# An attention kernel: fewer self-waits on ScalarE, a cheaper exp in the planner's table, one DMA transpose a head, first K and Q pieces in PSUM banks of their own

The kernel runs on one core of one Trainium2 chip. The metric is device time in microseconds, lower is better.

## The reference

Grouped-query attention: 8 batches, 8 query heads on 2 key/value heads, 1024 positions, head dimension 64, fp32 in and out.

```python
scores = scale * np.matmul(q_group, k_group.transpose(0, 1, 3, 2))
attn = np.exp(scores - scores.max(axis=-1, keepdims=True))
attn = attn / (np.sum(attn, axis=-1, keepdims=True) + 1e-08)
output[:, q_start:q_end] = np.matmul(attn, v_group)
```

## The kernel before

The work is cut into 128 jobs (batch, head, half of the queries) of 8 cells each; a cell is a 128x512 block of transposed scores, so there are 1024. The exponential of a cell is made on one of two engines. On ScalarE ("A" cells) it is the engine's own exponential, two cells a tile (128x1024). On VectorE ("D" cells) it is a bit trick with a quadratic correction, in groups of 8 cells. The maximum is not subtracted; a column of ones in V gives the row sums.

A planner at build time divides the cells and fixes the order of every engine's instructions, with a table of costs. The order is then static.

```python
QK, PV, P1, NORM = 0.216, 0.1225, 0.603, 0.555
EXP = (0.065, 0.4265)               # fixed part, and for each cell of the tile
... PER_JOB, LEAD, RAMP, AHEAD, FIRST_PV = ... 3, 6, 6, 0.08, 2.0
...
def exps(n, cells):                 # one A tile
    pt = pa_pool.tile([128, 2, QBS], BF16, name="pa")     # 28 buffers
    nc.scalar.activation(out=pt[:, 0:m], in_=psum.pop(("A", n))[:, 0:m],
                         func=AF.Exp, scale=scale)
...
def transpose(key, dst, n):         # PIECE = 256: two a head
    rows = slice(n * PIECE, (n + 1) * PIECE)
    nc.sync.dma_start_transpose(out=dst[:, rows], in_=src[rows, :])
...
# first loads: head 0 is turned on TensorE; both halves of K in one PSUM bank
tk = dbanks[0].tile([128, 2, HALF], BF16, name="dps0")
for n, half in enumerate(halves):
    ...                             # casts, transposes
for copy, half in zip((nc.scalar.copy, nc.vector.tensor_copy), halves):
    put_k(0, 0, half)
    copy(out=qT[(0, 0)][:, cols], in_=tq[:, cols])
turn_k(1, slice(0, NHC))
put_k(0, 1, slice(0, NHC))
nc.gpsimd.dma_start(out=ksets[0][hi, 0, 1, :], in_=ksets[0][lo, 0, 0, :])
```

A tile that is written into a used buffer waits for its readers (PE) and for its earlier writer, which is ScalarE itself. With both waits the build puts a separate wait instruction ahead of the exp.

Of the kernel before, what the change touches and what calls it, by code (L numbers as in the profile page):

```python
# [14 lines left out]
GROUP = 8  # L15
POOL_STEPS = ()


def make_plan(nj, nkc):
# [8 lines left out]
    EXP = (0.065, 0.4265)  # L28
    CHAIN = ((0.20, 0.133), (0.20, 0.133), (0.16, 0.27), (0.16, 0.27))
    FROM_PE, FROM_ACT, FROM_DVE, FROM_POOL = 0.26, 0.17, 0.10, 0.15  # L30
    LIVE_A, LIVE_D, PENDING, PER_JOB, LEAD, RAMP, AHEAD, FIRST_PV = 28, 5, 16, 3, 6, 6, 0.08, 2.0
    INF = 1e9
    FIRST_LOAD, EACH_LOAD = 4.5, 4.2
    ops = []
    pe = act = dve = 0.0
    a_free, bank, obank_free = [0.0, 0.0], [0.0, 0.0], [0.0, 0.0]
    todo = [list(range(nkc)) for _ in range(nj)]
    taken = [0] * nj
    job_a = job_d = 0
# [8 lines left out]
    def loaded(j):  # L48
        h = j // 2
        return FIRST_LOAD + EACH_LOAD * (h - 1 if h < 4 else h) if h else 0.0  # L50

    def first_free(slots):
        return min(range(len(slots)), key=lambda s: slots[s])

    while normed < nj:
# [27 lines left out]
        if len(open_jobs) < 2 and next_job < nj:  # L83
            at = min(ready.get(next_job * nkc + c, INF) for c in range(nkc))
            at = max(pe, FIRST_PV, min(obank_free), at)
            if at < INF:
                best = min(best or (INF,), (at, 3 + len(open_jobs), "open", next_job))
        for q, p, kind in ((normq, 0, "norm"), (p1q, 1, "p1"), (chainq, 2, "chain")):
            if q:
                at = q[0][0]  # L90
                if kind != "chain" or q[0][3] not in POOL_STEPS:
                    at = max(dve, at)
                best = min(best or (INF,), (at, p, kind, 0))
# [3 lines left out]
        if kind == "qk":  # L97
# [4 lines left out]
            if not arg:  # L102
                if open_a is None:
                    slot = first_free(a_free)
                    a_id += 1
                    live["A"] += 1
                    open_a = {"slot": slot, "t": a_free[slot], "cells": []}
                    a_free[slot] = INF
                o = open_a
                ops.append((t, "qk", cell, "A", a_id, o["slot"], len(o["cells"])))  # L110
                o["cells"].append(cell)
                home[cell] = ("A", a_id)
                if len(o["cells"]) == 2 or not any(todo[job_a:]):
                    act = max(act, pe + FROM_PE)
                    ops.append((act, "exp", a_id, tuple(o["cells"])))
                    act += EXP[0] + EXP[1] * len(o["cells"])
                    a_free[o["slot"]] = act + FROM_ACT
                    uses[("A", a_id)] = len(o["cells"])
                    for x in o["cells"]:
                        ready[x] = act + FROM_ACT  # L120
                    open_a = None
            else:
                taken[j] += 1
                k = first_free(bank)
                bank[k] = INF
                pending += 1
                ops.append((t, "qk", cell, "D", k, 0, 0))
                p1q.append((pe + FROM_PE, cell, k))
# [7 lines left out]
        elif kind == "pv":  # L136
# [11 lines left out]
            if done:  # L148
                open_jobs.remove(s)
                normq.append((pe + FROM_PE, s))  # L150
# [6 lines left out]
        elif kind == "p1":  # L157
            _, cell, k = p1q.pop(0)
            if not cur:
                d_id += 1  # L160
                live["D"] += 1
            ops.append((t, "p1", cell, k, d_id, len(cur)))
            dve = t + P1
            bank[k] = dve + FROM_DVE
            cur.append(cell)
            home[cell] = ("D", d_id)
            if len(cur) == GROUP:
                chainq.append((dve + FROM_DVE * (0 in POOL_STEPS), d_id, cur, 0))
                cur = []
        elif kind == "flush":  # L170
            chainq.append((dve + FROM_DVE * (0 in POOL_STEPS), d_id, cur, 0))
            cur = []
        else:
            _, g, cells, step = chainq.pop(0)
            ops.append((t, "chain", g, len(cells), step))
            end = t + CHAIN[step][0] + CHAIN[step][1] * len(cells)
            dve = end if step not in POOL_STEPS else dve
            if step + 1 < len(CHAIN):
                at = end
                if (step in POOL_STEPS) != (step + 1 in POOL_STEPS):  # L180
                    at += FROM_POOL if step in POOL_STEPS else FROM_DVE
                chainq.insert(0, (at, g, cells, step + 1))
            else:
                pending -= len(cells)
                uses[("D", g)] = len(cells)
                for x in cells:
                    ready[x] = dve + FROM_DVE
# [4 lines left out]
def kernel(  # L192
# [27 lines left out]
    PIECE = 256  # L220
    WARM = 30
    CAST_GAP = 3.0
    POOL_DMA = 1.0
    scale = 1.0 / math.sqrt(D)
# [10 lines left out]
    for op in plan:  # L235
        if op[1] == "chain" and op[4] in POOL_STEPS:
            starts.setdefault(op[2], []).append(op[0])
# [9 lines left out]
    pa_pool = ctx.enter_context(tc.tile_pool(name="papool", bufs=28))  # L247
# [14 lines left out]

    blank = const_pool.tile([128, 128], BF16)
# [77 lines left out]
    def first_loads():  # L341
# [7 lines left out]
        tk = dbanks[0].tile([128, 2, HALF], BF16, name="dps0")  # L349
        lo, hi = slice(0, D), slice(D, 2 * D)  # L350

        def turn_k(w, half):
            for c in range(NHC)[half]:
                nc.tensor.transpose(  # L354
                    tk[:, w, c * 128 : (c + 1) * 128],
# [4 lines left out]
        def put_k(side, parity, half):  # L360
# [4 lines left out]
                in_=tk[part, side ^ parity, cols],  # L365
# [19 lines left out]
        tq = dbanks[1].tile([128, HALF], BF16, name="dps1")  # L385
        qT[(0, 0)] = qT_pool.tile([128, HALF], BF16, name="qT")
        last_score[0] = keep_warm(WARM)
        for n, half in enumerate(halves):
# [5 lines left out]
            turn_k(0, half)  # L394
            keep_warm(2)
            for c in range(NHC)[half]:
                nc.tensor.transpose(tq[:, c * 128 : (c + 1) * 128], hq[:, c, :], ident)  # L397
# [3 lines left out]
        for copy, half in zip((nc.scalar.copy, nc.vector.tensor_copy), halves):  # L401
            cols = slice(half.start * 128, half.stop * 128)
            put_k(0, 0, half)
            copy(out=qT[(0, 0)][:, cols], in_=tq[:, cols])
        turn_k(1, slice(0, NHC))
        last_score[0] = keep_warm(4)
        put_k(0, 1, slice(0, NHC))
# [5 lines left out]
    temps = {}  # L413
    stage = {}
# [19 lines left out]
    def exps(n, cells):  # L434
        pt = pa_pool.tile([128, 2, QBS], BF16, name="pa")
        m = len(cells)
        nc.scalar.activation(  # L437
            out=pt[:, 0:m], in_=psum.pop(("A", n))[:, 0:m], func=AF.Exp, scale=scale
        )
        for col, cell in enumerate(cells):  # L440
# [15 lines left out]
    def exp_curve(g, m, step):  # L456
        pd = groups[g][:, 0:m]
        eng = nc.gpsimd if step in POOL_STEPS else nc.vector
        if step == 0:
            z = tmp_pool.tile([128, GROUP, QBS], U16, name="z")[:, 0:m]  # L460
            temps[g] = [z]
# [3 lines left out]
        elif step == 1:  # L465
            y = tmp_pool.tile([128, GROUP, QBS], FP16, name="y")[:, 0:m]
            temps[g].append(y)
            eng.tensor_scalar(  # L468
                out=y,
                in0=temps[g][0],  # L470
# [5 lines left out]
        elif step == 2:  # L476
            z, y = temps[g]
            eng.tensor_tensor(out=y, in0=z, in1=y, op=ALU.mult)  # L478
        else:
            y = temps.pop(g)[1]  # L480
            groups.pop(g)
            eng.tensor_tensor(out=pd, in0=pd, in1=y, op=ALU.add)  # L482
# [120 lines left out]
```

## Time and profile before

| | us |
|---|---|
| median of 3 runs | 393.23 (392.59 to 393.68) |
| span of the profiled execution | 390.84 |
| first exp starts / fourth exp starts | 6.76 / 10.26 |
| last exp ends | 386.35 |
| from there to the end of the span (the tail) | 4.49 |
| ScalarE, VectorE, PE busy | 97%, 94%, 93% |

The exp starts and ends are read from the single records of the trace. The prediction shows the views on which the rest stands. Among them is the chain that ended last: the profile follows it back from the last instruction, at each step to what released it or to the instruction before it on its engine, and each line of it gives the start and the length in us. "issue" in it is time in which the engine waited for nothing that the profile shows.

### The profile page before, as it was taken

The numbers are of one execution on the slowest core, as the hardware profiler recorded it, in microseconds if no ns is written. First come the engines' busy times: TensorE is split into PE (matmuls) and PEld (weight loads), VectorE is DVE, ScalarE is ACT, GpSimd is POOL, SyncE is SP. The second block draws the span as 40 slices with busy tenths as digits, with TensorE's granted clock in tenths as the row PEclk, the third lists the DMA queues.
The fourth block names the chain that finished last, engine by engine and source line by source line (L and its number), as shares of the span: only waits on it lengthen the run. The fifth ranks groups of instructions, "written<-read, shape, count | busy, mean of one in ns | idle before, by whom it ended". The sixth has DMA issues, their size and how long they took to land.

```text
span 390.8 us, 12423 instructions
## 1 busy us (share of the span) xinstructions
PE 363.8 (93%) x5081; PEld 233.9 (60%) x5172; DVE 366.4 (94%) x573; ACT 380.6 (97%) x415; POOL 111.1 (28%) x185
## 2 busy tenths in 40 slices
PE   7988999999999999999999999999999999999995
PEld 5434656656566666656566566566566566566564
DVE  4999999999999999999999999999999999999993
ACT  5999999999999999999999999999999999999995
POOL 5463340514205133331501425132243313200000
PEclk9999999999999999999999999999999999999999
DMA  7696987776939559693936669569585745931113
GB/s 128 120 190 104 136 133 153 135 125 128 162 80 147 99 126 141 117 141 77 151 86 118 130 98 165 106 119 139 104 145 105 126 86 113 116 87 52 33 55 82
DMA packets 102040, 45.52 MB, mean 116 GB/s; under 512 B 66272, under 2 KB 99552, under 8 KB 100736
## 3 DMA queue, kind: packets, MB, share of 16 engines
q0 software_dynamic: 21648, 17.18, 34.8%
q1 hardware_dynamic: 79792, 27.29, 31.2%
q8 instruction: 40, 0.66, 0.7%
q10 hardware_dynamic: 544, 0.26, 0.2%
q14 instruction: 16, 0.13, 0.2%
HBM read 25.17 MB, written 27.00 MB: 133 GB/s over the span
## 4 chain that ended last, share of the span: by engine, by line
ACT 74%; PE 19%; issue 5%; DMA 1%; DVE 0%
ACT pa L437 74%; PE aps L426 8%; PE ops L490 6%; PE dps L426 3%; PE ops L381 1%; DMA kset<-kset 1%; DVE kset L363 0%; PE dps L354 0%; DVE ost L506 0%; DVE rec L503 0%; DVE blank L264 0%; PE dps L397 0%
## 5 line engine op out<-in xcount | busy, mean ns | idle before, releaser
L437 ACT ACTIVATE pa<-aps 128x1024 bf16<-128x1024 f32 x411 | 378.2, 1068 | 2.4 <-PE aps L426 1.7
L426 PE MATMUL aps<-qT,kset 128*128 128x512 bf16 x731 | 224.3, 378 | 16.1 <-ACT pa L437 14.6
L490 PEld LDWEIGHTS <-pa 128*128 128x128 bf16 x3288 | 136.6, 97 | 59.8
L490 PE MATMUL ops<-vset,pa 128*128 128x65 bf16 x3288 | 147.3, 194 | 2.9
L446 DVE TENSOR_SCALAR pd<-dps 128x512 uint16<-128x512 f32 x202 | 130.8, 683 | 4.8 <-PE dps L426 4.2
L426 PEld LDWEIGHTS <-kset 128*128 128x128 bf16 x1024 | 82.2, 97 | 70.4 <-issue 36.3
L299 POOL DMA_DIRECT2D scr_q<-in_q_dram x63 | 35.8, 568 | 197.6 <-PE aps L426 139.1
L426 PE MATMUL dps<-qT,kset 128*128 128x512 bf16 x202 | 70.0, 378 | 1.8 <-DMA kset<-kset 0.7
L506 DVE TENSOR_TENSOR ost<-ops,rec 128x256 f32<-128x256 f32 x128 | 54.3, 425 | 4.4
L482 DVE TENSOR_TENSOR pd<-pd,y 128x4096 uint16<-128x4096 uint16 (+1 forms) x26 | 57.8, 2223 | 0.3
L478 DVE TENSOR_TENSOR y<-z,y 128x4096 f16<-128x4096 uint16 (+1 forms) x26 | 57.7, 2221 | 0.1
L490 PEld LDWEIGHTS <-pd 128*128 128x128 bf16 x808 | 37.3, 97 | 21.1 <-DVE ost L506 0.5
L490 PE MATMUL ops<-vset,pd 128*128 128x65 bf16 x808 | 41.8, 193 | 0.7
L319 POOL DMA_DIRECT2D kset<-kT x60 | 34.6, 587 | 3.0 <-DMA kT<-scr_k 1.7
L468 DVE TENSOR_SCALAR y<-z 128x4096 f16<-128x4096 uint16 (+1 forms) x26 | 31.6, 1215 | 0.0
L462 DVE TENSOR_SCALAR z<-pd 128x4096 uint16<-128x4096 uint16 (+1 forms) x26 | 31.0, 1191 | 0.0
L503 DVE RECIPROCAL rec<-ops 128x4 f32<-128x4 f32 x128 | 22.7, 177 | 8.1 <-PE ops L490 6.9
L332 POOL DMA_DIRECT2D vset<-in_v_dram x32 | 28.8, 905 | 3.0 <-issue 3.0
L299 POOL DMA_DIRECT2D scr_k<-in_k_dram x15 | 7.8, 518 | 22.6 <-PE dps L426 10.2
L381 PE MATMUL ops<-blank 128*128 128x128 bf16 x40 | 4.5, 291 | 1.1 <-DVE blank L264 1.1
L381 PEld LDWEIGHTS <-blank 128*128 128x128 bf16 x40 | 3.9, 138 | 1.1 <-DVE blank L264 1.1
L339 POOL DMA_DIRECT2D kset<-kset x6 | 3.1, 529 | 0.0
(21 smaller groups left out, 10.2 us busy)
## 6 DMA issues: line engine op xcount, KB each, us to landing
out_dram<-ost SPq DMA_DIRECT2D x63, 256.0 KB, 3.3
scr_q<-in_q_dram POOLq DMA_DIRECT2D x63, 128.0 KB, 3.3
kset<-kT POOLq DMA_DIRECT2D x60, 64.0 KB, 3.5
vset<-in_v_dram POOLq DMA_DIRECT2D x32, 64.0 KB, 4.0
qT<-scr_q SPq DMA_TRANSPOSE x126, 4.0
scr_k<-in_k_dram POOLq DMA_DIRECT2D x15, 128.0 KB, 3.4
kset<-kset POOLq DMA_DIRECT2D x7, 128.0 KB, 4.8
kT<-scr_k SPq DMA_TRANSPOSE x30, 3.6
```

The lines of the kernel that those rows point to most:

```text
L299: dma = nc.gpsimd.dma_start(out=scr.rearrange("(p f) -> p f", f=1024), in_=src.rearrange("(p s) d -> p (s d)", s=1024 // D),)
L319: nc.gpsimd.dma_start(out=ksets[b % 2][side * D : (side + 1) * D, g, side, parity * HALF : (parity + 1) * HALF], in_=kT[(b, g)][parity * D ...
L332: nc.gpsimd.dma_start(out=vsets[b % 2][:, g, two * NHC : (two + 1) * NHC, 0:D], in_=v[b, g].rearrange("(c p two) d -> two p c d", p=128, t ...
L426: last_score[0] = nc.tensor.matmul(dst, lhsT=ksets[b % 2][:, h // HPG, side, c * 128 : (c + 1) * 128], rhs=qT[(b, h)], start=True, stop=Tr ...
L437: nc.scalar.activation(out=pt[:, 0:m], in_=psum.pop(("A", n))[:, 0:m], func=AF.Exp, scale=scale)
L446: nc.vector.tensor_scalar(out=groups[g][:, slot], in0=psum.pop(cell), scalar1=bits_scale, scalar2=bits_bias, op0=ALU.mult, op1=ALU.add,)
L462: eng.tensor_scalar(out=z, in0=pd, scalar1=0x7F, scalar2=None, op0=ALU.bitwise_and)
L468: eng.tensor_scalar(out=y, in0=temps[g][0], scalar1=CURVE_A / 128.0, scalar2=CURVE_B, op0=ALU.mult, op1=ALU.add,)
L478: eng.tensor_tensor(out=y, in0=z, in1=y, op=ALU.mult)
L482: eng.tensor_tensor(out=pd, in0=pd, in1=y, op=ALU.add)
L490: nc.tensor.matmul(ops_of[s][:, qs, :], lhsT=p_of[cell][:, qs * 128 : (qs + 1) * 128], rhs=vsets[b % 2][:, h // HPG, c, :], start=opens an ...
L506: nc.vector.tensor_tensor(out=stage[(b, h)][:, :, side, :], in0=o[:, :, 0:D], in1=rec.unsqueeze(2).to_broadcast([128, NQS, D]), op=ALU.mult,)
```

## The change

Its intent: ScalarE sets the end, so take the wait on itself away from most exp tiles, let the planner know that an exp is now cheaper, start earlier, and issue fewer transposes. The 28 buffers become one ring; one exp in 8 waits for an exp that covers the next 8.

```diff
-    EXP = (0.065, 0.4265)
+    EXP = (0.05, 0.4268)
-    ... PER_JOB, LEAD, RAMP, AHEAD ... = ... 3, 6, 6, 0.08
+    ... PER_JOB, LEAD, RAMP, AHEAD ... = ... 2, 6, 6, 0.04
+    FIRST_TURN = 3.3        # when the second half of head 0 is there
-    PIECE = 256
+    PIECE = 512
+    OBSERVE = 8
-        pt = pa_pool.tile([128, 2, QBS], BF16, name="pa")
+        pt = p_ring[:, n % P_TILES]
-        nc.scalar.activation(...)
+        act = nc.scalar.activation(...)
+        exp_ins.append(act.ins)
+        if n >= P_TILES and n % OBSERVE == 0:
+            seen = exp_ins[n - P_TILES + OBSERVE - 1]
+            tc.add_manual_dep(act.ins, seen.name, SYNC, reason="ring")
-        tk = dbanks[0].tile([128, 2, HALF], BF16, name="dps0")
+        tk = [dbanks[0].tile([128, HALF], ...), apools[1].tile([128, HALF], ...)]
-        tq = dbanks[1].tile([128, HALF], BF16, name="dps1")
+        tq = [dbanks[1].tile([128, HALF], ...), obanks[0].tile([128, HALF], ...)]
+            # inside the loop over halves
+            if n == 0:
+                put_k(0, 0, half, n)
+            else:
+                nc.vector.tensor_copy(out=qT[(0, 0)][:, cols], in_=tq[n][:, cols])
+                nc.scalar.copy(out=ksets[0][lo, 0, 0, :HALF][:, cols], in_=tk[n][lo, cols])
+        nc.scalar.copy(out=qT[(0, 0)][:, : HALF // 2], in_=tq[0][:, : HALF // 2])
```

Cut from the diff: renamed constants, the planner's delays between engines (`FROM_PE` 0.26 to 0.21, and 0.16 after an output matmul; `FROM_ACT` 0.17 to 0.165), and a way to split the correction's steps that is not used.

More of the change, by code (lines that the diff above doesn't have):

```diff
@@ L13, with part @@
 CURVE_A, CURVE_B = 0.32988085, -0.33401025
-GROUP = 8
-POOL_STEPS = ()
+A_CELLS, D_BANKS, O_BANKS = (2, 2), 2, 2
+GROUP, PARTS = 8, 2
+CHAIN = ("and", "line", "prod", "add")
+ON_POOL = ()
+def part(step, m):
+    n = step[-1]
+    return slice(0, m) if not n.isdigit() else slice(m * int(n) // PARTS, m * (int(n) + 1) // PARTS)
 def make_plan(nj, nkc):
     QK, PV, P1, NORM = 0.216, 0.1225, 0.603, 0.555
-    EXP = (0.065, 0.4265)
-    CHAIN = ((0.20, 0.133), (0.20, 0.133), (0.16, 0.27), (0.16, 0.27))
-    FROM_PE, FROM_ACT, FROM_DVE, FROM_POOL = 0.26, 0.17, 0.10, 0.15
-    LIVE_A, LIVE_D, PENDING, PER_JOB, LEAD, RAMP, AHEAD, FIRST_PV = 28, 5, 16, 3, 6, 6, 0.08, 2.0
+    EXP = (0.05, 0.4268)
+    FOUR, TWO = (0.20, 0.133), (0.16, 0.27)
+    COST = {"and": FOUR, "line": FOUR, "prod": TWO, "add": TWO}
+    FROM_PE, FROM_PV, FROM_ACT, FROM_DVE, FROM_POOL = 0.21, 0.16, 0.165, 0.10, 0.15
+    LIVE_A, LIVE_D, PENDING, PER_JOB, LEAD, RAMP, AHEAD, FIRST_PV = 28, 5, 16, 2, 6, 6, 0.04, 2.0
     INF = 1e9
-    FIRST_LOAD, EACH_LOAD = 4.5, 4.2
+    FIRST_TURN, FIRST_LOAD, EACH_LOAD = 3.3, 4.5, 4.2
     ops = []
     pe = act = dve = 0.0
-    a_free, bank, obank_free = [0.0, 0.0], [0.0, 0.0], [0.0, 0.0]
+    a_free, bank, obank_free = [0.0] * len(A_CELLS), [0.0] * D_BANKS, [0.0] * O_BANKS
     todo = [list(range(nkc)) for _ in range(nj)]
@@ L49, in loaded @@
         h = j // 2
-        return FIRST_LOAD + EACH_LOAD * (h - 1 if h < 4 else h) if h else 0.0
+        if not h:
+            return FIRST_TURN * (j % 2)
+        return FIRST_LOAD + EACH_LOAD * (h - 1 if h < 4 else h)
     def first_free(slots):
@@ L82, in make_plan @@
                     best = min(best or (INF,), (at, 3 + i, "pv", (s, c)))
-        if len(open_jobs) < 2 and next_job < nj:
+        if len(open_jobs) < O_BANKS and next_job < nj:
             at = min(ready.get(next_job * nkc + c, INF) for c in range(nkc))
@@ L90, in make_plan @@
                 at = q[0][0]
-                if kind != "chain" or q[0][3] not in POOL_STEPS:
+                if kind != "chain" or CHAIN[q[0][3]] not in ON_POOL:
                     at = max(dve, at)
@@ L112, in make_plan @@
                 home[cell] = ("A", a_id)
-                if len(o["cells"]) == 2 or not any(todo[job_a:]):
+                if len(o["cells"]) == A_CELLS[o["slot"]] or not any(todo[job_a:]):
                     act = max(act, pe + FROM_PE)
@@ L149, in make_plan @@
                 open_jobs.remove(s)
-                normq.append((pe + FROM_PE, s))
+                normq.append((pe + FROM_PV, s))
         elif kind == "norm":
@@ L167, in make_plan @@
             if len(cur) == GROUP:
-                chainq.append((dve + FROM_DVE * (0 in POOL_STEPS), d_id, cur, 0))
+                chainq.append((dve, d_id, cur, 0))
                 cur = []
         elif kind == "flush":
-            chainq.append((dve + FROM_DVE * (0 in POOL_STEPS), d_id, cur, 0))
+            chainq.append((dve, d_id, cur, 0))
             cur = []
@@ L174, in make_plan @@
             _, g, cells, step = chainq.pop(0)
-            ops.append((t, "chain", g, len(cells), step))
-            end = t + CHAIN[step][0] + CHAIN[step][1] * len(cells)
-            dve = end if step not in POOL_STEPS else dve
+            ops.append((t, "chain", g, len(cells), CHAIN[step]))
+            name = CHAIN[step]
+            fixed, each = COST[name.rstrip("0123456789")]
+            end = t + fixed + each * len(cells[part(name, len(cells))])
+            dve = end if name not in ON_POOL else dve
             if step + 1 < len(CHAIN):
                 at = end
-                if (step in POOL_STEPS) != (step + 1 in POOL_STEPS):
-                    at += FROM_POOL if step in POOL_STEPS else FROM_DVE
+                if (name in ON_POOL) != (CHAIN[step + 1] in ON_POOL):
+                    at += FROM_POOL if name in ON_POOL else FROM_DVE
                 chainq.insert(0, (at, g, cells, step + 1))
@@ L219 @@
     E1 = D + 1
-    PIECE = 256
+    PIECE = 512
     WARM = 30
     CAST_GAP = 3.0
+    P_TILES = 28
     POOL_DMA = 1.0
+    OBSERVE = 8
     scale = 1.0 / math.sqrt(D)
@@ L235 @@
     for op in plan:
-        if op[1] == "chain" and op[4] in POOL_STEPS:
+        if op[1] == "chain" and op[4] in ON_POOL:
             starts.setdefault(op[2], []).append(op[0])
@@ L246 @@
     kT_pool = ctx.enter_context(tc.tile_pool(name="kTpool", bufs=4))
-    pa_pool = ctx.enter_context(tc.tile_pool(name="papool", bufs=28))
     pd_pool = ctx.enter_context(tc.tile_pool(name="pdpool", bufs=5))
@@ L261 @@
     apools, dbanks, obanks = psum_pools("aps", 2), psum_pools("dps", 2), psum_pools("ops", 2)
+    p_ring = const_pool.tile([128, P_TILES, 2, QBS], BF16)
     blank = const_pool.tile([128, 128], BF16)
@@ L348, in first_loads, with turn_k @@
         hk = first_pool.tile([128, NHC, 3, D], BF16, name="hk")
-        tk = dbanks[0].tile([128, 2, HALF], BF16, name="dps0")
+        tk = [
+            dbanks[0].tile([128, HALF], BF16, name="dps0"),
+            apools[1].tile([128, HALF], BF16, name="aps1"),
+        ]
         lo, hi = slice(0, D), slice(D, 2 * D)
-        def turn_k(w, half):
+        def turn_k(w, half, bank):
             for c in range(NHC)[half]:
                 nc.tensor.transpose(
-                    tk[:, w, c * 128 : (c + 1) * 128],
+                    tk[bank][:, c * 128 : (c + 1) * 128],
                     hk[:, c, w : w + 2, :].rearrange("p w d -> p (w d)"),
@@ L358, in turn_k, with put_k @@
                 )
-        def put_k(side, parity, half):
+        def put_k(side, parity, half, bank):
             part = (lo, hi)[side]
@@ L364, in put_k @@
                 out=ksets[0][part, 0, side, parity * HALF : (parity + 1) * HALF][:, cols],
-                in_=tk[part, side ^ parity, cols],
+                in_=tk[bank][part, cols],
             )
@@ L384, in first_loads @@
         hq = first_pool.tile([128, NHC, 2 * D], BF16, name="hq")
-        tq = dbanks[1].tile([128, HALF], BF16, name="dps1")
+        tq = [
+            dbanks[1].tile([128, HALF], BF16, name="dps1"),
+            obanks[0].tile([128, HALF], BF16, name="ops0"),
+        ]
         qT[(0, 0)] = qT_pool.tile([128, HALF], BF16, name="qT")
@@ L393, in first_loads @@
             nc.vector.tensor_copy(out=hk[:, half, 2, :], in_=fk[:, half, 0, :])
-            turn_k(0, half)
+            turn_k(0, half, n)
             keep_warm(2)
             for c in range(NHC)[half]:
-                nc.tensor.transpose(tq[:, c * 128 : (c + 1) * 128], hq[:, c, :], ident)
+                nc.tensor.transpose(tq[n][:, c * 128 : (c + 1) * 128], hq[:, c, :], ident)
             if n == 0:
@@ L400, in first_loads @@
                 cast(("q", 0, 2), q[0, 2])
-        for copy, half in zip((nc.scalar.copy, nc.vector.tensor_copy), halves):
             cols = slice(half.start * 128, half.stop * 128)
-            put_k(0, 0, half)
-            copy(out=qT[(0, 0)][:, cols], in_=tq[:, cols])
-        turn_k(1, slice(0, NHC))
+            if n == 0:
[4 more added lines that the diff above has]
+        nc.scalar.copy(out=qT[(0, 0)][:, : HALF // 2], in_=tq[0][:, : HALF // 2])
+        turn_k(1, slice(0, NHC), 0)
         last_score[0] = keep_warm(4)
-        put_k(0, 1, slice(0, NHC))
+        put_k(0, 1, slice(0, NHC), 0)
         nc.gpsimd.dma_start(out=ksets[0][hi, 0, 1, :], in_=ksets[0][lo, 0, 0, :])
@@ L413 @@
     temps = {}
+    exp_ins = []
     stage = {}
@@ L434, in exps @@
     def exps(n, cells):
-        pt = pa_pool.tile([128, 2, QBS], BF16, name="pa")
+        pt = p_ring[:, n % P_TILES]
         m = len(cells)
-        nc.scalar.activation(
+        act = nc.scalar.activation(
             out=pt[:, 0:m], in_=psum.pop(("A", n))[:, 0:m], func=AF.Exp, scale=scale
         )
+        exp_ins.append(act.ins)
+        if n >= P_TILES and n % OBSERVE == 0:
+            seen = exp_ins[n - P_TILES + OBSERVE - 1]
+            tc.add_manual_dep(act.ins, seen.name, SYNC, reason="ring")
         for col, cell in enumerate(cells):
@@ L456, in exp_curve @@
     def exp_curve(g, m, step):
-        pd = groups[g][:, 0:m]
-        eng = nc.gpsimd if step in POOL_STEPS else nc.vector
-        if step == 0:
-            z = tmp_pool.tile([128, GROUP, QBS], U16, name="z")[:, 0:m]
-            temps[g] = [z]
+        eng = nc.gpsimd if step in ON_POOL else nc.vector
+        if g not in temps:
+            z = tmp_pool.tile([128, GROUP, QBS], U16, name="z")
+            y = tmp_pool.tile([128, GROUP, QBS], FP16, name="y")
+            temps[g] = z, y
+        cells = part(step, m)
+        pd, z, y = groups[g][:, cells], temps[g][0][:, cells], temps[g][1][:, cells]
+        if step.startswith("and"):
             eng.tensor_scalar(
@@ L464, in exp_curve @@
             )
-        elif step == 1:
-            y = tmp_pool.tile([128, GROUP, QBS], FP16, name="y")[:, 0:m]
-            temps[g].append(y)
+        elif step.startswith("line"):
             eng.tensor_scalar(
                 out=y,
-                in0=temps[g][0],
+                in0=z,
                 scalar1=CURVE_A / 128.0,
@@ L475, in exp_curve @@
             )
-        elif step == 2:
-            z, y = temps[g]
+        elif step.startswith("prod"):
             eng.tensor_tensor(out=y, in0=z, in1=y, op=ALU.mult)
         else:
-            y = temps.pop(g)[1]
+            eng.tensor_tensor(out=pd, in0=pd, in1=y, op=ALU.add)
+        if step == CHAIN[-1]:
+            temps.pop(g)
             groups.pop(g)
-            eng.tensor_tensor(out=pd, in0=pd, in1=y, op=ALU.add)
     def output_mms(s, cell, opens, closes, bk):
```

## The prediction

> **What bounds the kernel now.** I began with the busy shares. Five engines work at once; ScalarE is the fullest, and it does one thing: the exponential of 411 tiles of 128x1024 scores. The costliest groups of instructions and the chain that ended last agree:
>
> ```profile
> PE 363.8 (93%) x5081; PEld 233.9 (60%) x5172; DVE 366.4 (94%) x573; ACT 380.6 (97%) x415; POOL 111.1 (28%) x185
> ACT 74%; PE 19%; issue 5%; DMA 1%; DVE 0%
> L437 ACT ACTIVATE pa<-aps 128x1024 bf16<-128x1024 f32 x411 | 378.2, 1068 | 2.4 <-PE aps L426 1.7
> ```
>
> 378.2 us over 411 tiles is 0.920 us a tile; one tile lasts 1068 ns by its record, so neighbours overlap by about 150 ns. ScalarE is idle for 2.4 us in front of these tiles, and nearly all of that lies in the first 10 us. The time is then three pieces: a head, 411 exps in a row, and a tail. From the records of the tiles the first exp starts at 6.76 us and the last one ends at 386.35; the span is 390.84, so the tail is 4.49.
>
> The decisive question is what the self-wait costs, and the kernel before contains its own control. The view of the exp line shows
>
> ```profile
> L437 ACT ACTIVATE pa<-aps x411: 1017/1074/1150, 6.8 to 385.3; 128x1024 bf16<-128x1024 f32 x137
> L437 ACTq EVENT_SEMAPHORE  x383: 17/17/17, 33.2 to 385.2; - x192
> ```
>
> The separate wait instruction of 17 ns is there for 383 tiles only, from 33.2 us on: the first 28 tiles write fresh buffers and have no self-wait. So I compared two runs of 12 tiles in the order of time, one before 33.2 us and one after:
>
> ```profile
> 12.17 11.10 ACT L437 ACTIVATE pa<-aps 128x1024 bf16<-128x1024 f32 x12
> 109.81 11.16 ACT L437 ACTIVATE pa<-aps 128x1024 bf16<-128x1024 f32 x12
> ```
>
> They take the same time. With the single records I can be exact. Without the self-wait the starts are first 904 ns apart, and the durations grow by 12 to 13 ns a tile, from 1017 to 1150; then the starts slow to 917. The ends are 917 ns apart all the while. With the self-wait the starts scatter between 904 and 925, the durations between 1017 and 1091, and the ends are again 917 apart: 381 of the 410 end-to-end distances lie between 914 and 919. So 904 ns is how fast ScalarE can accept tiles, 917 ns how fast it finishes them, and the sustained rate is the second one, with or without the self-wait. What the wait takes away is lead: ScalarE starts a tile at best 1091 ns ahead of its end, not 1150.
>
> All distances between ends that exceed 917 add up to 2.74 us. That is all that can be won between first and last exp without changing the number of tiles: 0.76 at the fourth tile (head), 1.34 at six tiles exactly 64 tiles apart (41, 105, ... 361), where the exp starts 0.32 to 0.35 us after its wait instruction where 0.045 is usual, and some 0.6 in fourteen small ones.
>
> **What the Trainium skill says.** "Perfetto Trace Analysis", section "Per-instruction lifecycle", has the hardware wait queue ahead of the engine, and a ScalarE record that runs from the start in the ALUs to the acknowledged write. That fits: the 17 ns wait runs in the sequencer while the exp before it is still at work, so it is hidden, and records overlap. "ScalarE: Activation LUTs", section "What ACT_TABLE_LOAD costs", gives 186 ns + 0.833 ns an element for immediate scale and bias and an overlap of about 93 ns: 946 ns for 1024 elements. The trace has 917, which decides; the element part, 853 ns, leaves a fixed 64 ns. "Runtime: NRT & Kernel Launch", section "Instruction fetch mechanics", has instructions refilled in blocks of 256 and the crossing "mostly hidden". The six hiccups are 128 recorded ScalarE instructions apart (64 exps, 64 waits); I take them for a refill, but by the trace the distance is shorter and about 0.2 us shows each time.
>
> **The change, part by part.** I built both programs and compared their order; this is no timing.
>
> 1. Self-waits: 383 become 52. Gain in steady rate: 383 x 0 = 0, by the comparison above. Gain in lead: some 50 to 60 ns a tile, which removes small stalls (ten of about 30 ns: 0.3 us). Fewer instructions: ScalarE then has about 474 (9 ahead, 413 exps, 52 waits) against some 800. If a hiccup comes every 128, as at instructions 63, 191, ... 703 now, there are four in place of six, each about 0.05 shorter: 4 x 0.17 = 0.7 against 1.34. With the 0.24 of a single disturbance around tile 187, I let the stalls after the head fall from 2.0 to about 1.1 us, a gain of 0.9; new ones can appear, as PE's order is new.
>
> 2. The division of work. The schedule is computed at build time from a cost table, where an exp of two cells now costs 0.9036 in place of 0.918, close to the 904 that I hold for a spacing of starts. So it gives ScalarE more: DVE has 199 cells in place of 202, ScalarE 825 in place of 822, that is 412 whole tiles and one half tile. Cost: 1 x 0.917 + one half tile (0.427 + 0.064 = 0.49) = 1.41 us more on the engine that sets the end. DVE wins some 4 us, which is off the path.
>
> 3. Head. In the chain of waits the fourth exp stands behind a DMA that copies K to the other half of the partitions:
>
> ```profile
> 6.10 0.43 DVE kset L363
> 6.81 2.30 DMA kset<-kset
> 9.16 0.39 PE dps L426
> 9.55 0.24 PE ops L490 x8
> 9.79 0.45 PE aps L426 x2
> 10.26 22.97 ACT pa L437 x25
> ```
>
> With banks of their own, the first K copies no longer wait for the second half of the transposes, and one moves to ScalarE. Following the copies with the present durations (DVE 0.24 to 0.29 each, ScalarE 0.37, PE transposes 0.38 for four), the last K copy starts near 5.9, not 6.10, and the DMA lands near 8.9, not 9.1. More important is PE's order: behind the landing now stand a DVE score, eight output matmuls, then the two scores of the exp (0.15 + 0.5 us after landing); in the new order those scores are next in line. The fourth exp starts near 8.95 + 0.22 + 0.42 = 9.6, a gain of 0.65.
>
> 4. Tail. In the new order, 18 groups of four output matmuls stand behind the last score (12 now), and the last exp is a half tile. From the last score's start, PE needs 0.22 + 18 x 0.12 = 2.4 us; ScalarE needs 0.87 + 0.49 = 1.36. PE then ends 1.0 us after the last exp, where it ends 0.49 after it now: a loss of 0.5. Normalising and the last store (4.0) stay.
>
> 5. One DMA transpose in place of two a head: halves the issues on the sync queue (126 + 30 become about 78). No PE wait for these tiles shows in the waits now, so I count 0. The copy arrives whole, but its second piece came last before too.
>
> Sum: -0.9 + 1.41 - 0.65 + 0.5 = +0.4 us on 393.23: 393.6. Since 1 may be worth a little more than I counted (lead also softens stalls that I put down as unavoidable), I say 393.4.
>
> **Rivals.** (a) Removing the wait brings the rate to 904 ns, as the new cost table holds. For it: 904 is the most frequent spacing of starts. Then 413 x 0.0126 = 5.2 us go, and the time is near 388.4, still within 2%. Against it: the first 28 tiles have no self-wait, yet settle at 917. I give it one chance in fifteen. (b) PE becomes the bound: it is busy 93%, and a slot of scores is refilled only after its exp ends. Score, wake-up and score again take 743 ns from the end of an exp to the start of the one two later; up to about 810 is free. The new plan lets other matmuls in front of A scores a little more readily (0.04 in place of 0.08), and has 18 places with two DVE scores and a group of outputs between exps where there were 7. If half of those stalled by 0.1, the time would be near 395. Against it: without the wait instruction that refill path gets some 50 ns shorter. (c) A whole-head transpose arrives late for the first heads, when the DMA engines are over 90% busy: one stall of 0.5 to 1.5 us, near 394.5. Against it: the second halves landed at 11.1 and 15.0 and no wait shows.
>
> **Range and chances.** The three runs before spread by 1.1 us; the terms above by about 0.5 each. Together I take 391.8 to 394.9 as eight in ten. Two per cent is 7.9 us: more than all idle time of ScalarE with rival (a) on top, and for a slowdown every tenth tile would have to stall by 0.2 us. Same: 0.98, the rest split.
>
> **What would show it.** Right: ends of exps 917 ns apart in the new trace too, durations up to about 1150; 413 exps, 52 separate waits; mean busy time an exp still near 0.918; the fourth exp near 9.6; four hiccups in place of six; a longer wait of the tail for output matmuls. Wrong: ends 904 apart (rival a), many ScalarE idle gaps ended by score matmuls (rival b), or a PE wait on a transposed Q (rival c).

## More of the kernel before

One more view is needed later, the DMA queues that fetch instructions (columns: packets, MB, share of the 16 engines' time):

```profile
q8 instruction: 40, 0.66, 0.7%
...
q14 instruction: 16, 0.13, 0.2%
```

0.66 MB in 40 packets are 16 KiB each, 0.13 MB in 16 packets 8 KiB each.

## The result, and the profile after

Changed: 393.19 us median of 4 runs (392.99 to 393.66). Before, in the same rounds: 393.31 (392.59 to 393.68). Ratio 1.0001, 95% interval 0.9984 to 1.0018: the same. A ratio here is the mean time of one kernel's fast runs over the mean of the other's of the same rounds, so it is not quite the ratio of the medians quoted.

First the page of the changed kernel: busy shares, the chain that ended last by engine, and the exp group (busy us, mean ns of one, idle us before them):

```profile
PE 369.5 (94%) x5172; PEld 233.4 (60%) x5172; DVE 362.6 (93%) x565; ACT 381.4 (97%) x418; POOL 109.3 (28%) x185
...
ACT 93%; PE 3%; DMA 1%; issue 1%; DVE 0%; SPq 0%; POOLq 0%
...
L463 ACT ACTIVATE p_ring<-aps 128x1024 bf16<-128x1024 f32 x413 | 378.7, 1098 | 1.1 <-PE aps L452 1.1
```

The chain now runs 93% along ScalarE where it was 74%. That share follows the wait instructions and says little about how late the scores come: it is 94% in e1 below, which has the PE order of before and only lacks most waits, and 64% in e2, which has the new order and all the waits, yet takes only some 0.4 us more than the changed kernel. The two lines of their pages:

```profile
ACT 94%; PE 3%; issue 1%; DMA 1%; DVE 0%
```

```profile
ACT 64%; PE 27%; issue 5%; DVE 3%; DMA 1%; POOLq 0%
```

The busy time of the exps rose from 378.2 to 378.7 with one tile and a half one more; for a whole tile it is 0.918 us, 0.920 before. Next the view of the exp line, and a run of 12 tiles in the order of time:

```profile
L463 ACT ACTIVATE p_ring<-aps x413: 700/1095/1151, 6.4 to 384.8; 128x1024 bf16<-128x1024 f32 x138
L463 ACTq EVENT_SEMAPHORE  x52: 17/17/17, 32.4 to 381.1; - x52
```

```profile
108.75 11.22 ACT L463 ACTIVATE p_ring<-aps 128x1024 bf16<-128x1024 f32 x12
```

383 separate waits became 52. The first of the 12 tiles lasts 1.135 us by its record, so the other eleven end within 11.22 - 1.135 = 10.085 us, 0.917 each: the rate did not move. The chain of waits at the start shows the earlier fourth exp:

```profile
6.60 2.38 DMA kset<-kset
8.98 0.05 issue
9.02 0.62 PE aps L452 x2
9.64 0.02 issue
9.66 22.80 ACT p_ring L463 x25
```

The two scores of the exp follow the landing at once; before, a VectorE score and eight output matmuls stood between. At the end it is the other way round. Before:

```profile
384.76 0.22 PE aps L426
384.98 0.05 issue
385.04 1.81 PE ops L490 x48
```

Changed:

```profile
384.22 0.32 PE aps L452
384.53 2.23 PE ops L522 x72
```

After the last score there are 72 output matmuls in the changed kernel against 48, and they end 1.23 us after the last exp (0.48 before). The last stores then come closer together: the three DMA issues start at 386.47, 386.89 and 387.48 by their records, 384.55, 386.40 and 387.54 before, and the part from PE's end to the end of the span grows from 4.01 to 4.47. This is the plan's and no accident of one profile: e2 and e6 below, with the same plan, have 1.24 for the first and 4.46 and 4.49 for the second, and all kernels with another plan 0.35 to 0.48 and 3.89 to 4.02. The timelines of the sync queue, before and then changed, show the same three issues merged:

```profile
384.55 3.36 SPq L515 DMA_DIRECT2D out_dram<-ost  x3
```

```profile
386.47 1.50 SPq L547 DMA_DIRECT2D out_dram<-ost  x3
```

With this the whole span can be accounted for. "Exp work" is the number of tiles from the fourth on by 0.9167 us (half tile 0.49); "stalls" is what is left up to the end of the last exp.

| us | before | changed | difference |
|---|---|---|---|
| fourth exp starts | 10.26 | 9.66 | -0.60 |
| exp work (408 tiles; 409 and a half one) | 374.01 | 375.42 | +1.41 |
| stalls | 2.08 | 0.43 | -1.65 |
| tail | 4.49 | 5.71 | +1.22 |
| span | 390.84 | 391.22 | +0.38 |

So the change gained 2.25 us and gave 2.63 back in these two profiles; the two are equal within the scatter of the runs. The experiments ask what made each line.

### The profile page after: what moved, and what is told of

It is laid out like the page before. It is cut to its first block, busy times and chain, and to the rows that moved or that the text cites. A ratio compares the mean times of both kernels' runs of the same rounds, so it can differ in the third digit from the quotient of the medians.

```text
span 391.2 us, 12065 instructions
## 1 busy us (share of the span) xinstructions
PE 369.5 (94%) x5172; PEld 233.4 (60%) x5172; DVE 362.6 (93%) x565; ACT 381.4 (97%) x418; POOL 109.3 (28%) x185
## 4 chain that ended last, share of the span: by engine, by line
ACT 93%; PE 3%; DMA 1%; issue 1%; DVE 0%; SPq 0%; POOLq 0%
ACT p_ring L463 93%; PE ops L522 2%; PE aps L452 1%; DMA fk<-in_k_dram 1%; DMA kset<-kset 1%; SPq L389 0%; DVE ost L538 0%; ACT hk L411 0%; DVE kset L382 0%; DVE qT L427 0%; PE aps L373 0%; DVE rec L535 0%; PE ops L419 0%; PE ops L400 0%; POOLq L433 0%
## 5 line engine op out<-in xcount | busy, mean ns | idle before, releaser
L463 ACT ACTIVATE p_ring<-aps 128x1024 bf16<-128x1024 f32 x413 | 378.7, 1098 | 1.1 <-PE aps L452 1.1
L452 PE MATMUL aps<-qT,kset 128*128 128x512 bf16 x825 | 244.6, 378 | 15.8 <-ACT p_ring L463 13.9
L522 PEld LDWEIGHTS <-p_ring 128*128 128x128 bf16 x3300 | 138.9, 97 | 63.7 <-DVE ost L538 0.3
L522 PE MATMUL ops<-vset,p_ring 128*128 128x65 bf16 x3300 | 150.1, 194 | 0.1
L477 DVE TENSOR_SCALAR pd<-dps 128x512 uint16<-128x512 f32 x199 | 129.5, 682 | 5.2 <-PE dps L452 5.0
L452 PE MATMUL dps<-qT,kset 128*128 128x512 bf16 x199 | 69.0, 378 | 0.0
L509 DVE TENSOR_TENSOR y<-z,y 128x4096 f16<-128x4096 uint16 (+1 forms) x25 | 56.8, 2270 | 0.0
L522 PEld LDWEIGHTS <-pd 128*128 128x128 bf16 x796 | 35.8, 97 | 19.5 <-DVE ost L538 2.2
L347 POOL DMA_DIRECT2D vset<-in_v_dram x32 | 26.9, 843 | 2.1 <-issue 2.1
L354 POOL DMA_DIRECT2D kset<-kset x6 | 5.0, 835 | 0.0
```

The costliest lines, as they stand in the source:

```text
L347: nc.gpsimd.dma_start(out=vsets[b % 2][:, g, two * NHC : (two + 1) * NHC, 0:D], in_=v[b, g].rearrange("(c p two) d -> two p c d", p=128, t ...
L452: last_score[0] = nc.tensor.matmul(dst, lhsT=ksets[b % 2][:, h // HPG, side, c * 128 : (c + 1) * 128], rhs=qT[(b, h)], start=True, stop=Tr ...
L463: act = nc.scalar.activation(out=pt[:, 0:m], in_=psum.pop(("A", n))[:, 0:m], func=AF.Exp, scale=scale)
L477: nc.vector.tensor_scalar(out=groups[g][:, slot], in0=psum.pop(cell), scalar1=bits_scale, scalar2=bits_bias, op0=ALU.mult, op1=ALU.add,)
L509: eng.tensor_tensor(out=y, in0=z, in1=y, op=ALU.mult)
L522: nc.tensor.matmul(ops_of[s][:, qs, :], lhsT=p_of[cell][:, qs * 128 : (qs + 1) * 128], rhs=vsets[b % 2][:, h // HPG, c, :], start=opens an ...
```

## The experiments

All kernels gave correct results, except the fourth. Its output is wrong, which doesn't matter for the time. Each but the fourth was timed against the kernel before in its own rounds, so two experiments of different rounds are best compared by their ratios. "Excess" below is what the distances between ends of exps, from the first to the last, have over 917 ns in sum (over 490 for a half tile).

| run | median us | ratio to before (95%) |
|---|---|---|
| e1 ring alone | 392.11 | 0.9981 (0.9969 to 0.9993) |
| e2 wait at each | 393.62 | 1.0016 (1.0004 to 1.0028) |
| e3 exp cost 0.07 | 391.02 | 0.9946 (0.9934 to 0.9958) |
| e5 before, one instruction more | 392.03 | 0.9974 (0.9962 to 0.9987) |
| e6 wait at each, one more | 395.04 | 1.0048 (1.0034 to 1.0061) |
| e7 exp cost 0.08 | 391.21 | 0.9957 (0.9944 to 0.9969) |
| e8 exp cost 0.10 | 395.35 | 1.0057 (1.0044 to 1.0070) |
| e9 head alone | 391.99 | 0.9971 (0.9959 to 0.9984) |
| e10 transposes alone | 392.77 | 0.9992 (0.9979 to 1.0006) |
| e11 exp cost 0.063 | 391.42 | 0.9958 (0.9946 to 0.9970) |
| e12 before, two more | 393.17 | 1.0002 (0.9989 to 1.0015) |

### Does the self-wait cost rate? (e4, e1, e2)

e4 replaces the whole body by exps on scores that lie ready:

```diff
+    for n in range(60): exp(ring[:, n], scores[...])        # no wait
+    for n in range(60): exp(ring[:, n], scores[...])        # self-wait alone
+    for n in range(60):                                     # self-wait and a second one
+        mark = nc.vector.memset(small[:, n : n + 1], 0.0)
+        e = exp(ring[:, n], scores[...]); tc.add_manual_dep(e.ins, mark.ins.name, ...)
+    ...                                                     # 128x512, 128x2048, from SBUF
```

> Wrong result on purpose: nothing but exps, on scores that lie ready in PSUM, so no engine can hold them up. Five stretches: 60 exps of 128x1024 with no wait; 60 with a self-wait that is the only wait; 60 with a self-wait and a wait on VectorE (so with the separate wait instruction); 60 of 128x512; 30 of 128x2048; 60 from SBUF. My theory: ends 917 ns apart in the first three alike; 128x512 at 917-427 = 490, 128x2048 at 1770 (a fixed 64 ns and 0.833 ns an element). Rival (ScalarE could do 904 and something else in the kernel holds it at 917): 904 in the first stretch. Rival (the self-wait costs): first stretch 904, third 917 or more.

Measured: mean distance of ends 916.6 ns without a wait, 916.7 with the self-wait, 916.7 with the separate wait instruction; 490.0 for 128x512, 1770.0 for 128x2048, and 934.3 from SBUF. The groups by shape (count, busy us and mean ns) and the view of the line:

```profile
L236 ACT ACTIVATE ring<-scores 128x1024 bf16<-128x1024 f32 x180 | 165.1, 2198 | 1.4 <-PE scores L228 1.4
```

```profile
L236 ACT ACTIVATE ring<-scores x270: 1018/2798/5445, 3.4 to 245.5; 128x1024 bf16<-128x1024 f32 x90, 128x512 bf16<-128x512 f32 x30, 128x2048 bf16<-128x2048 f32 x15
L236 ACTq EVENT_SEMAPHORE  x60: 17/17/17, 102.5 to 156.6; - x60
```

165.1 us over 180 tiles is 0.917 each, with and without the wait: the rival of 904 ns is out. The second fence corrects my own reading. With nothing to hold ScalarE up, the recorded starts of 128x1024 exps are 903 to 904 ns apart through all three stretches, and the durations grow by 13 ns a tile, to 3392 ns at the end of the third; the 5445 of the fence was reached later, in the 128x2048 stretch. I take it that an engine isn't several tiles ahead of itself, so the start stamp drifts in a run of back-to-back exps; in any case "904 is how fast ScalarE can accept tiles", as the prediction had it, is not shown. Only the ends are a measure. What can still be read from a start is how soon after a score it comes: from the second score's start to the exp's, the shortest was 413 ns in the changed kernel; the usual one before was about 475.

e1 is the kernel before with the ring and its wait at every eighth tile, with the very same order on PE:

```diff
-        pt = pa_pool.tile([128, 2, QBS], BF16, name="pa")
+        pt = p_ring[:, n % 28]
+        if n >= 28 and n % 8 == 0:
+            tc.add_manual_dep(act.ins, exp_ins[n - 21].name, SYNC, reason="ring")
```

> The kernel before with the self-wait part of the change alone; plan, PE order, head and transposes are those of before. My theory (exps finish 917 ns apart with or without the self-wait; the wait only takes lead, and the refetch of instructions shows only where the sequencer itself waits): ends still 917 apart, the excess over 917 between the first and the last end falls from 2.74 us to about 1.1 (0.8 of it at the fourth exp), the hiccups 64 tiles apart vanish, time 391.5 to 392.2, ratio about 0.996. Rival (the wait costs 13 ns a tile): 5 us less, near 388. Rival (the stalls vanished in the changed kernel because of the new PE order, not the wait): no change, 393.3.

Measured: 392.11 us, 0.8 less than before in the same rounds. The excess of the ends over 917 fell to 1.36 us, of which 0.8 is the fourth and fifth exp. The theory's size held roughly, and the hiccups 64 tiles apart are gone, but one of 0.27 us is there at tile 48. Tile 48 is one of those that still have a wait instruction.

e2 puts the self-wait back into the changed kernel:

```diff
-    OBSERVE = 8
+    OBSERVE = 1
```

> The changed kernel with the self-wait back at each exp tile from the 29th on (384 tiles in place of 52), all else as changed. My theory: ends still 917 apart; hiccups of some 0.2 us come back 64 tiles apart, with small stalls; 1.0 to 1.7 us slower than the changed kernel, 394.2 to 394.9. Rival (the wait costs 13 ns a tile): 5 us slower, near 398. Rival (PE order): no change.

My theory failed here. 384 waits are back, but no hiccup of 0.2 us came 64 tiles apart; the excess is 1.07 us against 0.81, in small stalls, and the time is 393.62, some 0.4 above the changed kernel (the intervals overlap). So 332 extra waits cost about half a microsecond or less, and the hiccups need something else. One rival fits so far, that the new PE order has none; e6 tests it.

### What are the hiccups? (e5, e6, e12, e9)

In the kernel before, each hiccup sat on the 63rd, 191st, 319th ... ScalarE instruction of the trace (counted from 0), and this instruction was an exp whose wait instruction was the last one of the block before it. In e1 it was the same for tile 48. In e2 the changed head has one ScalarE copy more, so the same place falls on a wait instruction. e5 adds just that to the kernel before:

```diff
+        extra = first_pool.tile([128, 8], BF16, name="extra")
+        nc.scalar.copy(out=extra, in_=blank[:, 0:8])
```

> The kernel before with one tiny ScalarE copy (128x8) more, at a place where ScalarE idles for its first loads; nothing else. Theory, formed after the first runs: a hiccup of 0.2 us comes where a block of 128 ScalarE instructions ends between the separate wait instruction and the exp that belongs to it; one instruction more puts the block's end ahead of the wait instruction, where it is hidden. Then the six hiccups go and the time falls by 1.0 to 1.4 us, to about 391.7 (ratio 0.9967). Rival (the hiccups come from the PE order or from PSUM slots of before): six hiccups at the same tiles and no change.

Measured: 392.03, that is 1.13 less, and no hiccup is left. The chain of waits around one of them, before:

```profile
103.17 1.10 ACT pa L437
104.27 0.10 issue
104.37 0.59 ACT pa L437
104.96 0.33 issue
105.29 0.80 ACT pa L437
```

and in e5, whose tiles stand 0.5 us later by then:

```profile
103.63 0.88 ACT pa L439
104.50 0.04 issue
104.54 0.87 ACT pa L439
105.41 0.05 issue
105.46 0.86 ACT pa L439
```

Before, the exp at 104.37 starts 0.10 us after the one before it has ended, and the next link is again cut by 0.33; in e5 the same tiles follow one another in 0.04 to 0.05.

e6 does the same to e2:

> The changed kernel with the self-wait at each exp tile, as in the second run, and the same tiny ScalarE copy. That run had no hiccup. Theory (where the block ends): six hiccups 64 tiles apart come back, the time rises by 1.0 to 1.4 us over that run, to about 394.8. Rival (the new PE order has no hiccups): 393.6 as in the second run.

Measured: 395.04, 1.4 more than e2 (1.3 by the ratios, as the rounds differ), with six hiccups at tiles 40, 104, 168, 232, 296 and 360. So it was not the new order that had removed them. e12 is the control, with two copies in place of one:

```diff
+        extra = first_pool.tile([128, 2, 8], BF16, name="extra")
+        for n in range(2):
+            nc.scalar.copy(out=extra[:, n], in_=blank[:, 8 * n : 8 * n + 8])
```

> Control for the fifth run: the kernel before with two tiny ScalarE copies in place of one. Theory (what counts is whether a block of 128 instructions ends between a wait instruction and its exp): with an even number more, the ends fall between the two again, one exp earlier; six hiccups near tiles 40, 104, ... 360 and the time of before, 392.8 to 393.3. Rival (the copy itself helps, for instance by loading the exponential's table earlier or by shifting the head): no hiccup, about 392.0.

Measured: 393.17, ratio 1.0002, excess 2.74 us, as before to the hundredth, and the hiccups are back at tiles 40, 104, 168 and on. The second of them:

```profile
104.05 0.09 issue
104.14 0.60 ACT pa L440
104.75 0.32 issue
```

So it is not the copy but the count. That the cause is the fetch of the next instructions is an inference, with this support from the trace of the kernel before: 8192-byte packets of an instruction queue start at 46.1, 105.3, 164.0, 223.7, 282.1 and 342.4 us, each 0.7 to 2.0 us after the start of a delayed exp (45.4, 104.4, 163.3, 222.4, 281.4, 340.4). e2 has such packets at the like places (46.0, 103.5, 162.3 and on) and no hiccup, so the fetch can be hidden. The packets start after the delayed exp, so they are not what it waited for; they only mark that something is fetched at this place. What is shown is the place in the count; the mechanism is not.

e9 takes the new first loads alone. It has that one copy more too, so it shows how two parts of a change can be mixed:

> The kernel before with the new first loads alone (first K and Q pieces in banks of their own, one K copy on ScalarE); plan, waits and transposes as before. The new code has one ScalarE instruction more, so by the fifth run's finding the six hiccups go too: 1.1 us. The head itself, without the new PE order, should give some 0.2 us (the last K copy earlier). Sum: 391.7 to 392.0, and no hiccup in the trace. Rival (the head alone brings its 0.65): 391.4 or less. Rival (the hiccups hang on something else than the count of instructions): six hiccups, 393.0.

Measured: 391.99, no hiccup; against e5 (392.03) the head itself brought nothing, and its fourth exp starts at 10.86, as in e1 (10.85) and e5 (10.95). In the kernels with the new head and the new PE order it starts at 9.66 (changed), 9.81 (e2), 10.10 (e6), 9.71 (e7), 10.11 (e8) and 9.77 (e11); only e3, with the same order of first scores, has 10.50. So the banks alone bring nothing measurable, and the gain is there where the new order is there too; the order without the new head was not run. Each figure is a single profile, and most of the scatter lies ahead of the first exp, which starts anywhere from 6.44 to 7.54. Counted from the first exp, the fourth comes 3.38 to 3.87 us later in the six kernels with the old order (3.40 in e9) and 3.07 to 3.27 later in the seven with the new one (3.15 in e3). So about 0.3 us goes with the new order (3.51 before, 3.22 changed). The other 0.32 of the ledger's 0.60 is an earlier first exp (6.44 against 6.76), which these profiles cannot tell from scatter.

### The transposes (e10)

```diff
-    PIECE = 256
+    PIECE = 512
```

> The kernel before with one DMA transpose for a head in place of two, nothing else. Theory: off the path, no change, 393.0 to 393.3, hiccups as before. Rival (a whole-head transpose comes late for the first heads): a wait of PE on a transposed Q, 0.5 us or more slower.

Measured: 392.77, ratio 0.9992, its interval holds 1. PE waits on no transposed Q, and once for 0.2 us on a copied K. Off the path, as predicted.

### The division and the tail (e3, e11, e7, e8)

Each is the changed kernel with another fixed part of an exp in the cost table:

```diff
-    EXP = (0.05, 0.4268)
+    EXP = (0.07, 0.4268)      # e3; 0.063 in e11, 0.08 in e7, 0.10 in e8
```

| | change | e11 | e3 | e7 | e8 |
|---|---|---|---|---|---|
| fixed part | 0.05 | 0.063 | 0.07 | 0.08 | 0.10 |
| cells on VectorE | 199 | 200 | 202 | 205 | 208 |
| exp tiles | 412.5 | 412 | 411 | 409.5 | 408 |
| groups of output matmuls behind the last score | 18 | 8 | 12 | 5 | 12 |
| excess, us | 0.81 | 0.76 | 0.66 | 3.22 | 7.93 |
| tail, us | 5.71 | 4.38 | 4.38 | 4.24 | 4.37 |
| median, us | 393.19 | 391.42 | 391.02 | 391.21 | 395.35 |

> The changed kernel with one number of the cost table set right: a two-cell exp costs 0.924 us there in place of 0.904 (fixed part 0.07). The division goes back to 202 cells on VectorE and 411 tiles on ScalarE, and 12 groups of output matmuls behind the last score in place of 18. My theory (the gain of the wait and the head went into 1.4 us more exp work and 1.2 us more tail): the last exp ends 1.4 us earlier, the tail shrinks from 5.7 to about 4.6, time 390.7 to 391.5, faster than both kernels by 0.4 to 0.6%. Rival (the new order, not the division, holds the time): within 0.3 us of the changed kernel.

e3's time came out as the theory had it: 391.02, less than both kernels by 0.5%. The last exp ends only 0.65 us earlier, though, in place of 1.4, as in this profile the first exp starts 0.91 later and the fourth 0.83; from the first exp to the last it takes 1.56 less. The tail shrank by 1.33. The chain at its end:

```profile
383.28 0.43 PE aps L452 x2
383.71 1.64 PE ops L522 x48
```

> The changed kernel with the fixed part of an exp at 0.063 in the cost table: 200 cells on VectorE and 412 whole exp tiles, nearly the change's 199 and 412 and a half; but 8 groups of output matmuls stand behind the last score, not 18. It tells tail from division: theory: 0.45 us less exp work and a tail of 4.3 to 4.5 in place of 5.7: 391.2 to 391.7. Rival (only the division counts, so the third run gained by its 202 cells): 392.7.

e11 tells the two apart. With nearly the change's division (half a tile less) it has a tail of 4.38, and the time is 391.42: within the range of the theory. Of the 1.77 us by which its median is below the change's, the half tile makes 0.49 and the tail 1.33. Against the kernel before, the ledger has the tail (1.22) and the extra exp work (1.41) at about the same size. The tail hangs on where the plan happens to end, not on the division as such.

> The changed kernel with the fixed part of an exp at 0.08 in the cost table (0.05 in the change, 0.07 in the third run): 205 cells on VectorE, 409 whole exp tiles and a half one, 5 groups of output matmuls behind the last score. If ScalarE sets the end: 1.5 x 0.917 = 1.4 us less than the third run (391.0), so 389.6 to 390.3. Rival (VectorE, 93% busy, or the matmuls behind it now hold ScalarE up): 391 or more, with ScalarE idle ahead of exps.

> The same with 0.10: 208 cells on VectorE, 408 exp tiles. If ScalarE still sets the end: 2.7 us less than the third run, near 388.4. VectorE then has 9 cells more than in the changed kernel, some 13 us more than its 362.6, so 376 us: nearly as much as ScalarE's 374. I expect that the two are about balanced and the stalls eat part of it: 388.5 to 391.

Both of these expectations failed. e7 has a tile and a half less than e3 and is no faster: the excess rose to 3.22 us. Its time is what the rival had, but the idle time ahead of exps that the rival looked for is only 1.1 us. In e8 the excess is 7.93, with 98 places over 8 ns. The groups and the waits of e8:

```profile
L463 ACT ACTIVATE p_ring<-aps 128x1024 bf16<-128x1024 f32 x408 | 381.1, 1037 | 1.8 <-PE aps L452 1.2
...
L477 DVE TENSOR_SCALAR pd<-dps 128x512 uint16<-128x512 f32 x208 | 134.9, 681 | 3.0 <-PE dps L452 2.8
```

```profile
PEld L522 <- DVE pd L511: 7.3, 13, 0.9
```

408 tiles are busy for 381.1 us, 0.934 each: the tiles come late one after the other by a little, which shows as longer distances and hardly as idle time. Two causes are possible: the planner believes that an exp takes 0.954 us and lets PE do that much other work between two tiles, and PE waits 7.3 us for VectorE's groups (2.2 in the changed kernel). The one number sets both the division and the pace, and no run changes one alone, but the trace of e8 speaks for the pace. Of its 97 late tiles from the fifth on (7.2 us of excess in all), only 13 (1.2 us) have a PE wait on VectorE between the start of the exp two before and the tile's last score. In 83 of the other 84, PE put four or more output matmuls or a VectorE score between the end of that exp and the last score; in tiles that came on time that is so in 71 of 222.

## Why the prediction was right

The predicted 393.4 us met 393.19, but two terms of the sum were each off by about 0.7 us, the stalls and the tail. They were off in opposite directions and cancelled, so that the number came so close is in part luck.

- **Rate: right, and the heart of it.** The self-wait costs no rate (e4). The comparison of the first 28 tiles with the later ones in the kernel before already showed it.
- **Stalls, -0.9 predicted, -1.65 measured.** The mis-sized term is "four in place of six, each about 0.05 shorter". No hiccup was left. The step assumed that every block's end costs; it costs only where the end parts a wait instruction from its exp. With 52 waits among 478 instructions no end did so, and even 384 waits would not have, as e2 shows. Either part would have done most of it alone: one instruction more with all the waits (e5, 1.13 us less), or 52 waits in place of 383 (e1, one hiccup in place of six, 0.8 us less). The other term, "ten of about 30 ns: 0.3 us" from the lead, fits e2, whose excess is 0.26 above the changed kernel's.
- **Division, +1.41: right**, by the counts of the build and the rate.
- **Head, -0.65 predicted, -0.60 measured** in the two profiles, of which only about 0.3 stands out from the scatter of the first exp's start. That the copies start earlier thanks to banks of their own gave nothing by itself (e9 against e5); the gain came only together with the reordered PE work, which was not run by itself.
- **Tail, +0.5 predicted, +1.22 measured.** PE ended 1.23 after the last exp, not 1.0. And "Normalising and the last store (4.0) stay" was wrong: it took 4.47. The last three stores were issued within 1.0 us in place of 3.0, and the last landed after 2.5 us in place of 2.0; that the one caused the other was not tested.
- **Transposes, 0: right** (e10).
- **The rivals.** 904 ns: ruled out by e4. PE as the bound: the stalls fell to 0.43 us, so the changed order did not hold ScalarE up (idle time alone would not tell, as e8 shows). Late transposes: no such wait.

The expected gain, then, went into three extra cells on ScalarE, because the cost table held 0.904, the most frequent distance of starts, as the cost of an exp, and into a plan that left PE with 18 groups at the end.

## What to carry to other kernels

Take an engine's sustained rate from the distance between ends in a run that nothing holds up, and look for a stretch of your own trace that already lacks the thing you want to remove. A cost table that divides work between engines should hold that rate: here 0.013 us too little for each tile gave the bound engine more work. When several parts change at once, write a ledger from head to tail; a time that stays the same may hide two microseconds each way.

## What the Trainium skill lacked or had wrong

- "ScalarE: Activation LUTs", section "What ACT_TABLE_LOAD costs": its 186 + 0.833·N less 93 ns overlap makes an estimate of 946 ns at 1024 elements, with no word on where the source lies. Measured back to back from PSUM: 490.0, 916.7 and 1770.0 ns for 512, 1024 and 2048, that is 63 + 0.833·N; from SBUF 934.3 at 1024.
- "Perfetto Trace Analysis", section "Per-instruction lifecycle": it says that a ScalarE record starts when the instruction starts in the ALUs. In back-to-back exps of 1024 elements the starts ran 13 ns a tile ahead of the ends, to durations of 3392 ns after 180 tiles (e4); they are no measure of occupancy or rate. Lacking: what a start means there.
- "Runtime: NRT & Kernel Launch", section "Instruction fetch mechanics": blocks of 256 instructions, mostly hidden. ScalarE's hiccups came every 128 recorded instructions, and the trace has both 16 KiB and 8 KiB instruction packets. Lacking: a block's end between a separate wait instruction and its exp cost 0.19 to 0.28 us, six times in the kernel before; one ScalarE instruction more took all six away (1.13 us).
- No page says what the separate wait instruction costs that two waits on one instruction bring: 17 ns in its record, nothing in rate (916.7 ns with it, 916.6 without).
